# The first 256 rows of a row-mean kernel: one load with two rows a partition instead of two loads with one, and means interleaved on chip

## The chip, the cores and the metric

One core of one Trainium2 chip. The metric is the device time of one execution in microseconds. A "run" below is one execution; a median is over the runs named.

## The reference

```python
def setup_inputs():
    batch, seq, dim = 32, 512, 1024
    return {"x": np.random.randn(batch, seq, dim).astype(np.float32)}

def reference(x):
    return np.mean(np.maximum(x, 0), axis=-1).astype(np.float32)
```

So 16,384 rows of 4 KB (67.11 MB) are read, and one number per row is written.

## The kernel before

Each row's ReLU and sum is one instruction, on ScalarE for even rows and on VectorE for odd ones, so the loads hold whole rows (only the last row of each partition comes in column pieces). The 256 first rows are treated apart, as two loads of 128 rows. Of the others each partition owns 126 consecutive ones, which come in seven loads of 16 rows a partition (8 MB each, in three buffers), then in shrinking pieces.

```python
    xfirst, xmain = xf[:2 * P, :].rearrange("(c p) d -> p c d", c=2), xf[2 * P:, :]
    ...
    for t in range(full):                       # full = 7, issued from SyncE
        buf_free(t)                             # waits for load t-3 to be consumed
        if t in (0, 2):
            c = t // 2
            load(c - 2, row0[:, c, :], xfirst[:, c, :])                 # 512 KB, 4 KB packets
        load(t, bufs[t % BUFS][:, :, :], xr[:, t * NB:(t + 1) * NB, :]) # 8 MB, 64 KB packets
        if t == BUFS + 2:
            nc.sync.wait_ge(first, 2)
            for c in range(2):                  # two stores of four 128-byte runs
                nc.sync.dma_start(
                    out=outfirst[c * P:(c + 1) * P].rearrange("(q i) -> q i", i=32), in_=turned0[c:P:32, :],
                ).then_inc(stored, 16)
    ...
    for t in range(full):                       # ScalarE and VectorE
        if t in (0, 2):
            c = t // 2
            nc.scalar.wait_ge(loaded[c - 2], 16)
            done = nc.scalar.activation(out=row0[:, c, :], in_=row0[:, c, :], func=ACT.Relu, scale=inv,
                                        accum_out=mean0[:, c:c + 1])
            if c == 1:
                done.then_inc(first, 1)
                nc.vector.wait_ge(first, 1)
                nc.vector.transpose(turned0[:, :], mean0[:, :]).then_inc(first, 1)
        rows(t, bufs[t % BUFS], 0, NB, t * NB)
    ...
    issue_ahead_of_entry_barrier(nc, 2)         # the first two loads are issued before the entry barrier
```

The entry barrier is the point at the program's start at which the engines wait for one another; the helper in the last line moves the first loads in front of it.

## Time and profile before

| | before |
|---|---|
| time, median of the first 3 runs | 161.39 us (161.09 to 161.4) |
| span in the profile | 159.8 us |
| VectorE, ScalarE busy | 46%, 44% |
| mean rate out of HBM over the span | 420 GB/s |

The lines on which the bound is read stand in the prediction. This is the timeline of SyncE's queue in the kernel before (start us, us, what is issued; merged lines):

```profile
0.00 0.39 SPq L109 DMA_DIRECT2D row<-in_x_dram  x1
0.43 1.82 SPq L109 DMA_DIRECT2D rows<-in_x_dram  x2
2.30 0.43 SPq L109 DMA_DIRECT2D row<-in_x_dram  x1
...
72.53 1.20 SPq L127 DMA_DIRECT2D out_dram<-turned  x2
```

The first 512 KB are issued at once and load 0 at 0.43 us. The second 512 KB follow at 2.30, between loads 1 and 2. And this is the DMA view:

```profile
GB/s 394 525 263 525 476 312 525 410 377 525 394 525 263 525 476 312 525 427 361 525 377 410 525 312 476 525 263 525 525 263 525 525 263 525 361 394 427 416 407 112
DMA packets 2608, 67.18 MB, mean 420 GB/s; under 512 B 560, under 2 KB 816, under 8 KB 1328
```

### The profile page before, as it was taken

Reading aid. Unit: us, or ns where it says so; the run is one execution under the profiler, and the core shown is the slowest. Engines: PE = TensorE matmul, PEld = TensorE weight load, DVE = VectorE, ACT = ScalarE, POOL = GpSimd, SP = SyncE. Lnnn points to the kernel's source line nnn. Section 1 sums busy time; section 2 is a strip of 40 time slices with the busy share of each in tenths; the row PEclk is TensorE's granted clock in tenths of the full one; section 3 lists DMA queues with packets and bytes.
Section 4 is the critical chain, followed back from the end, with each engine's and each line's share of the span. In section 5 each row is a group of like instructions: output and inputs, shape, how many; then the busy total and the mean of one; then the engine's idle time right before and its main releaser. Section 6 shows DMA issues by size and latency. Waiting matters only on the chain. (4 is left out here: it accounts for less than half of the span.)

```text
span 159.8 us, 350 instructions
## 1 busy us (share of the span) xinstructions
DVE 73.1 (46%) x131; ACT 70.3 (44%) x133; POOL 1.3 (1%) x9
## 2 busy tenths in 40 slices
DVE  0000029900499002990049800597007950089995
ACT  1400029800499002980049600595007930089974
POOL 1000000000000000000000000000000000000001
DMA  9969979989996997998989979969969969899993
GB/s 394 525 263 525 476 312 525 410 377 525 394 525 263 525 476 312 525 427 361 525 377 410 525 312 476 525 263 525 525 263 525 525 263 525 361 394 427 416 407 112
DMA packets 2608, 67.18 MB, mean 420 GB/s; under 512 B 560, under 2 KB 816, under 8 KB 1328
## 3 DMA queue, kind: packets, MB, share of 16 engines
q1 hardware_dynamic: 2608, 67.18, 98.0%
HBM read 67.11 MB, written 0.07 MB: 420 GB/s over the span
## 5 line engine op out<-in xcount | busy, mean ns | idle before, releaser
L20 DVE TENSOR_SCALAR_CACHE_REDUCE rows<-rows 128x1024 f32<-128x1024 f32 (+1 forms) x63 | 71.9, 1208 | 84.5 <-DMA rows<-in_x_dram 84.5
L15 ACT ACTIVATE rows<-rows 128x1024 f32<-128x1024 f32 (+1 forms) x63 | 65.2, 1034 | 83.9 <-DMA rows<-in_x_dram 83.8
L15 ACT ACTIVATION_READ_ACCUMULATOR rows<-rows 128x1 f32 x63 | 11.7, 186 | 0.0
L20 DVE DVE_READ_ACCUMULATOR rows<-rows 128x1 f32 x63 | 5.2, 83 | 0.0
L169 ACT ACT_TABLE_LOAD x1 | 1.3, 1283 | 3.4 <-DMA row<-in_x_dram 3.4
L169 ACT ACTIVATE row<-row 128x1024 f32<-128x1024 f32 x2 | 2.1, 1048 | 0.0
L159 POOL TENSOR_SCALAR res<-sums 128x112 f32<-128x112 f32 (+1 forms) x2 | 0.5, 244 | 153.9 <-DVE rows L20 153.9
L15 ACT ACTIVATE last<-last 128x512 f32<-128x512 f32 x1 | 0.6, 629 | 0.0
L20 DVE TENSOR_SCALAR_CACHE_REDUCE last<-last 128x256 f32<-128x256 f32 x1 | 0.4, 420 | 0.3 <-DMA last<-in_x_dram 0.3
L203 DVE SCALAR_TENSOR_TENSOR last<-last,scale 128x258 f32<-128x258 f32 x1 | 0.4, 428 | 0.1
L169 ACT ACTIVATION_READ_ACCUMULATOR row<-row 128x1 f32 x2 | 0.4, 186 | 0.0
L175 DVE STREAM_TRANSPOSE turned<-mean 128x32 f32<-128x32 f32 x1 | 0.2, 214 | 0.3 <-ACT row L169 0.3
L144 POOL MEMSET scale<- 128x258 f32 x1 | 0.3, 313 | 0.0
L193 POOL TENSOR_SCALAR res<-part 128x1 f32<-128x1 f32 x1 | 0.3, 265 | 0.5 <-DVE rows L20 0.5
L15 ACT ACTIVATION_READ_ACCUMULATOR last<-last 128x1 f32 x1 | 0.2, 186 | 0.0
L143 POOL MEMSET mean<- 128x32 f32 x1 | 0.1, 125 | 1.5 <-POOLq L55 1.5
L241 POOL MEMSET const-bfloat16-1.0<- 128x1 bf16 x1 | 0.1, 101 | 0.0
L241 POOL MEMSET const-uint8-127<- 128x1 uint8 x1 | 0.1, 101 | 0.0
L241 POOL MEMSET const-float32-0.0<- 128x1 f32 x1 | 0.1, 98 | 0.2 <-issue 0.2
L241 POOL MEMSET const-float32-1.0<- 128x1 f32 x1 | 0.1, 98 | 0.0
L20 DVE DVE_READ_ACCUMULATOR last<-last 128x1 f32 x1 | 0.1, 83 | 0.0
L203 DVE DVE_READ_ACCUMULATOR last<-last,scale 128x1 f32 x1 | 0.1, 82 | 0.0
## 6 DMA issues: line engine op xcount, KB each, us to landing
rows<-in_x_dram SPq DMA_DIRECT2D x1, 3072.0 KB, 36.7
rows<-in_x_dram SPq DMA_DIRECT2D x1, 2048.0 KB, 41.2
row<-in_x_dram SPq DMA_DIRECT2D x2, 512.0 KB, 22.3
rows<-in_x_dram SPq DMA_DIRECT2D x1, 1024.0 KB, 43.2
rows<-in_x_dram SPq DMA_DIRECT2D x1, 512.0 KB, 44.0
last<-in_x_dram SPq DMA_DIRECT2D x1, 256.0 KB, 44.3
last<-in_x_dram SPq DMA_DIRECT2D x2, 128.0 KB, 44.0
rows<-in_x_dram SPq DMA_DIRECT2D x7, 48.7
```

Of the source, the lines that this page charges most:

```text
L15: return nc.scalar.activation(out=src, in_=src, func=ACT.Relu, accum_out=acc)
L20: return nc.vector.tensor_scalar(out=src, in0=src, scalar1=0.0, scalar2=init, op0=ALU.max, op1=ALU.add, accum_out=acc,)
L143: nc.gpsimd.memset(mean0[:, :], 0.0)
L144: nc.gpsimd.memset(scale[:, :], inv).then_inc(pool, 1)
L159: nc.gpsimd.tensor_scalar(out=res[:, lo:hi], in0=sums[:, lo:hi], scalar1=inv, scalar2=0.0, op0=ALU.mult, op1=ALU.add,).then_inc(pool, 1)
L169: done = nc.scalar.activation(out=row0[:, c, :], in_=row0[:, c, :], func=ACT.Relu, scale=inv, accum_out=mean0[:, c:c + 1],)
L175: nc.vector.transpose(turned0[:, :], mean0[:, :]).then_inc(first, 1)
L193: nc.gpsimd.tensor_scalar(out=res[:, J - 2:J - 1], in0=part[:, 0:1], scalar1=part[:, 1:2], scalar2=inv, op0=ALU.add, op1=ALU.mult,).then_i ...
L203: nc.vector.scalar_tensor_tensor(out=last[:, 768:], in0=last[:, 768:], scalar=0.0, in1=scale[:, :], op0=ALU.max, op1=ALU.mult, accum_out=r ...
L241: nc = _bacc.Bacc("TRN2", target_bir_lowering=False, num_devices=1)
```

## The change

The intent: fewer and larger transfers. Partition p takes rows 2p and 2p+1, so both lie together in memory, and one load of 1 MB in packets of 8 KB replaces two of 512 KB in packets of 4 KB. The means then come in pairs, so after VectorE's transpose GpSimd interleaves them, and one store of four 256-byte runs replaces two stores of four 128-byte runs.

```diff
-    xfirst, xmain = xf[:2 * P, :].rearrange("(c p) d -> p c d", c=2), xf[2 * P:, :]
+    xfirst, xmain = xf[:2 * P, :].rearrange("(p c) d -> p c d", c=2), xf[2 * P:, :]
...
-        if t in (0, 2):
-            c = t // 2
-            load(c - 2, row0[:, c, :], xfirst[:, c, :])
+        if t == 0:
+            load(-1, row0[:, :, :], xfirst)
         load(t, bufs[t % BUFS][:, :, :], xr[:, t * NB:(t + 1) * NB, :])
-        if t == BUFS + 2:
-            nc.sync.wait_ge(first, 2)
-            for c in range(2):
-                nc.sync.dma_start(
-                    out=outfirst[c * P:(c + 1) * P].rearrange("(q i) -> q i", i=32), in_=turned0[c:P:32, :],
-                ).then_inc(stored, 16)
+        if t == BUFS:
+            nc.sync.wait_ge(first, 3)
+            nc.sync.dma_start(
+                out=outfirst.rearrange("(q i) -> q i", i=64), in_=runs0[0:P:32, :, :],
+            ).then_inc(stored, 16)
...
+    nc.scalar.wait_ge(loaded[-1], 16)
+    for c in range(2):
+        done = nc.scalar.activation(
+            out=row0[:, c, :], in_=row0[:, c, :], func=ACT.Relu, scale=inv, accum_out=mean0[:, c, 0:1],
+        )
+    done.then_inc(first, 1)
+    nc.vector.wait_ge(first, 1)
+    nc.vector.transpose(turned0[:, :, :], mean0[:, :, :]).then_inc(first, 1)
+    nc.gpsimd.wait_ge(first, 2)
+    nc.gpsimd.tensor_copy(out=runs0[:, :, :].rearrange("p i c -> p c i"), in_=turned0[:, :, :]).then_inc(first, 1)
     for t in range(full):
-        (the same for t in (0, 2), one row each)
         rows(t, bufs[t % BUFS], 0, NB, t * NB)
```

Cut: the larger tiles, one load semaphore fewer, and the final wait for three stores in place of four.

More of the change, by code (lines that the diff above doesn't have):

```diff
@@ L88 @@
     scale = sbuf("scale", P, D // 4 + 2)
-    row0, mean0, turned0 = sbuf("row0", P, 2, D), sbuf("mean0", P, 32), sbuf("turned0", P, 32)
-    loaded = [nc.alloc_semaphore(f"loaded{i}") for i in range(full + len(row_pieces) + len(col_pieces) + 2)]
+    row0, mean0 = sbuf("row0", P, 2, D), sbuf("mean0", P, 2, 32)
+    turned0, runs0 = sbuf("turned0", P, 2, 32), sbuf("runs0", P, 32, 2)
+    loaded = [nc.alloc_semaphore(f"loaded{i}") for i in range(full + len(row_pieces) + len(col_pieces) + 1)]
     act, dve, pool = (nc.alloc_semaphore(n) for n in ("act", "dve", "pool"))
@@ L140 @@
         c, i = c + w, i + 1
-    nc.gpsimd.memset(mean0[:, :], 0.0)
+    nc.gpsimd.memset(mean0[:, :, :], 0.0)
     nc.gpsimd.memset(scale[:, :], inv).then_inc(pool, 1)
@@ L164 @@
     nc.vector.wait_ge(pool, 1)
-    for t in range(full):
-        if t in (0, 2):
-            c = t // 2
-            nc.scalar.wait_ge(loaded[c - 2], 16)
-            done = nc.scalar.activation(
-                out=row0[:, c, :], in_=row0[:, c, :], func=ACT.Relu, scale=inv, accum_out=mean0[:, c:c + 1],
-            )
-            if c == 1:
-                done.then_inc(first, 1)
-                nc.vector.wait_ge(first, 1)
-                nc.vector.transpose(turned0[:, :], mean0[:, :]).then_inc(first, 1)
+    nc.scalar.wait_ge(loaded[-1], 16)
[8 more added lines that the diff above has]
+    nc.gpsimd.tensor_copy(out=runs0[:, :, :].rearrange("p i c -> p c i"), in_=turned0[:, :, :]).then_inc(first, 1)
+    for t in range(full):
         rows(t, bufs[t % BUFS], 0, NB, t * NB)
@@ L223 @@
     nc.switch_bb("rows_end")
-    nc.sync.wait_ge(stored, 64).then_inc(stored, -64)
+    nc.sync.wait_ge(stored, 48).then_inc(stored, -48)
     issue_ahead_of_entry_barrier(nc, 2)
```

## The prediction

> **What bounds the kernel now.** I started with the head of the page and the busy slices, to see which engine could be the bound.
>
> ```profile
> span 159.8 us, 350 instructions
> DVE 73.1 (46%) x131; ACT 70.3 (44%) x133; POOL 1.3 (1%) x9
> ...
> DMA  9969979989996997998989979969969969899993
> ...
> HBM read 67.11 MB, written 0.07 MB: 420 GB/s over the span
> ```
>
> No engine is half busy, while the DMA row reads 9 or nearly so from the first slice to the last but one. The dips to 6 are long packets counted in one slice. The kernel is a stream of 67.11 MB out of HBM, and the two arithmetic engines wait for it. The view of waits says the same:
>
> ```profile
> DVE rows L20 <- DMA rows<-in_x_dram: 84.5, 7, 23.0
> ACT rows L15 <- DMA rows<-in_x_dram: 83.8, 9, 17.0
> ```
>
> Columns: total us, times, longest. VectorE waits 84.5 us in seven waits, one for each 8 MB load. The chain that ended last is of no use here: it stops after half a microsecond, at the last VectorE instruction. So I read the landings of the loads from the timeline, where the first instruction after an idle stretch starts when its load has landed:
>
> ```profile
> 3.44 1.28 ACT L169 ACT_TABLE_LOAD   x1 [3.44 <-DMA row<-in_x_dram]
> ...
> 23.00 1.22 DVE L20 TENSOR_SCALAR_CACHE_REDUCE rows<-rows 128x1024 f32<-128x1024 f32 x1 [23.00 <-DMA rows<-in_x_dram]
> 42.24 1.22 DVE L20 TENSOR_SCALAR_CACHE_REDUCE rows<-rows 128x1024 f32<-128x1024 f32 x1 [10.04 <-DMA rows<-in_x_dram]
> 62.86 1.22 DVE L20 TENSOR_SCALAR_CACHE_REDUCE rows<-rows 128x1024 f32<-128x1024 f32 x1 [10.91 <-DMA rows<-in_x_dram]
> 82.21 1.22 DVE L20 TENSOR_SCALAR_CACHE_REDUCE rows<-rows 128x1024 f32<-128x1024 f32 x1 [10.14 <-DMA rows<-in_x_dram]
> ```
>
> The later ones start at 101.57, 120.92 and 140.25 in the same view. Where nothing but an 8 MB load lies between two landings the step is 19.35 us, and 8.389 MB / 19.35 us = 433.5 GB/s. Between 42.24 and 62.86 lies also the second small load of 512 KB (0.524 MB): the step is 20.62 us, 1.27 more. At 433.5 GB/s its bytes alone are 1.21 us, so its being a transfer of its own, in 4 KB packets, costs about **0.06 us**. The span is a head (about 1 us to the first packet), some 156 us of stream, and a tail of 2 to 3 us (last reduction, last store).
>
> **What the Trainium skill says.**
> 1. "DMA: Bandwidth & Descriptors", section "Where 436 GB/s comes from": the fabric into SBUF tops out at 435.2 GB/s, and HBM gives one core about 358. The trace agrees with the first: 433.5. It does not show the second as a limit for this one core.
> 2. Same page, "Why small descriptors are slow (HBM only)": each packet carries a fixed overhead. The records of single packets in the trace agree and give its size: a 4 KB packet takes 159 ns, 8 KB 309, 16 KB 612, 64 KB 2418. From 8 KB to 64 KB that is 0.0368 ns a byte, so about 8 ns of each packet are fixed.
> 3. Same page, "Rules for kernel authors": at least 1 MiB per DMA for bandwidth. That rule would favour the change (512 KB becomes 1 MB), but in this trace the 512 KB load lost only 0.06 us, because other loads stand in the queue on both sides of it.
> 4. "VectorE: DVE Perf Modes", "The three transpose paths": VectorE turns 32x32 blocks independently. The trace has the one used, 128x32 in 214 ns; the changed one has two such columns of blocks.
>
> **The change, part by part.**
>
> *Loads.* Two loads of 512 KB, 128 packets of 4 KB each, become one of 1 MB with 128 packets of 8 KB. The bytes are the same. Each of 16 engines moves 8 packets of 309 ns instead of 16 of 159: 2472 against 2544 ns, **0.07 us less** on the stream, which sets the end. One load fewer also saves one completion write of 9 ns per engine, 0.01 us. The issue of the second load (0.43 us of SyncE at 2.30) is off the path, since the queue holds an 8 MB load by then.
>
> *Order.* All 1 MB now lies ahead of load 0, so loads 0 and 1 land about 1.20 us later (24.1 and 43.4), and from load 2 on everything lands about 0.08 us earlier (62.78, 82.13, ...). Their buffers come free 1.2 us later: the issue of load 3, at 32.30 now, moves to about 33.5. Load 3's turn on the DMA engines comes at 62.8, so 29 us of slack remain.
>
> *Arithmetic on the first rows.* Two ScalarE activations (1.05 us + 0.19 each) stay. They move together, after a landing at about 4.6 and the table load of 1.28, so they end near 8.4 us. Then VectorE's transpose (one more column of blocks than 214 ns: I take 0.25), then a new GpSimd copy of 128x64. GpSimd's 128x112 instruction takes 286 ns and its 128x12 one 201, so 0.85 ns a column and 0.25 us for 64. The larger memset takes perhaps 0.03 us more. All is done by about 9.2 us, with VectorE and ScalarE idle until load 0 lands at 24.1. Before, the second activation and the transpose sat at 50.6 to 52.0, also in idle time. On the path: **0**.
>
> *Stores.* Two stores of four 128-byte runs become one of four 256-byte runs, issued after load 3 (near 33.8) instead of after load 5 (72.5). In the packet records the old ones ran at 120.05 to 120.2, behind load 5, at 13 ns a packet. The step from 120.92 to 140.25 that contains them is 19.33, no longer than others. Saving at most 0.02 us, if those engines are the slow ones. SyncE is spared one issue of about 0.6 us, off the path. The wait for the means (three signals) is met 24 us before SyncE comes to it.
>
> *Tail.* Load 6 and the pieces behind it shift by the same 0.08 us. VectorE works without a break from load 6's landing to 157.0 and then waits 0.3 us for the last column pieces. Both sides of that near-tie move together, so the shift passes through to the end.
>
> Sum: 0.07 + 0.01 + up to 0.02, about **0.1 us less**: 161.39 becomes **161.3 us**. That is 0.06%, below the spread of the three runs before (161.09 to 161.4).
>
> **Rivals.**
> - *The first load delays everything.* If load 0's landing 1.2 us later were not given back at load 2, the time would be 162.6. Against it: total bytes are unchanged and the queue never empties (steps of 19.35 throughout). For it only that load 0's landing does move.
> - *The new chain ScalarE, VectorE, GpSimd, SyncE becomes a wait that blocks the queue.* SyncE issues load 4 behind that store. Against: done near 9 us, needed at 33.8; even then load 4 has until 82. Cost 0. To cost anything it would have to take over 70 us.
> - *A full fixed cost per transfer is saved.* Were some 2 us of set-up and receipt exposed for each load, the gain would be 1 to 2 us, about 160.0. Against: the measured 0.06 us above.
> - *The ramp at the start.* The first packets of 4 KB take 355 to 638 ns instead of 159, while the rate builds up. If with 8 KB packets the ramp is better or worse used, I would put it at 0.1 to 0.2 us either way, 161.1 to 161.5. This is the largest real doubt, and it is as large as the effect.
>
> **Range and chances.** The mechanism gives 161.3; the ramp and the run-to-run spread of 0.3 us are larger than the gain. The range that should hold it 8 times in 10 is 160.9 to 161.7. A change of 2% is 3.2 us: nothing in the rivals reaches it. Faster 0.01, within 2% 0.98, slower 0.01.
>
> **What would show it.** Right: 2456 packets instead of 2608 (128 of data, 4 of stores and 20 completion writes fewer) and under 8 KB 1048 instead of 1328; loads 0 and 1 landing at about 24.1 and 43.4, loads 2 to 6 about 0.08 us earlier than before; steps between landings still 19.35; the copy on GpSimd over by 10 us; load 3 issued near 33.5 without the queue running dry; the waits of VectorE for loads still near 84 us. Wrong: load 2 landing later than 62.9, a step other than 19.35 where the store now runs (load 3 to load 4), or SyncE held at its wait for the means. A span that differs by over 0.4 us would mean that the head or the tail does something that I have not seen.

## The result, and the profile after

After: **161.25 us**, median of 6 runs (161.15 to 161.34). Before, in the runs beside it: 161.16 us, median of 6 (160.98 to 161.4). Ratio 1.0003, 95% interval 0.999 to 1.0016: the same. A ratio here is the mean time of one kernel's runs over that of the other's of the same rounds, so it is not quite the ratio of the medians quoted.

The page and the DMA view of the kernel after:

```profile
span 159.9 us, 349 instructions
DVE 73.1 (46%) x131; ACT 70.3 (44%) x133; POOL 1.6 (1%) x10
GB/s 248 539 525 262 525 525 262 525 525 262 525 508 279 525 459 328 525 361 426 525 263 525 525 262 525 525 262 525 525 262 525 525 262 525 361 394 426 414 407 114
DMA packets 2456, 67.18 MB, mean 420 GB/s; under 512 B 536, under 2 KB 792, under 8 KB 1048
```

The packet counts are the predicted ones (2456 and 1048). The first GB/s slice falls from 394 to 248, which looks like a much slower start and is not one. The single-packet records show that the first 16 packets of 64 KB start from 2.5 us on before and from 4.2 on after; in a slice of 4.0 us 16 such packets are 262 GB/s. The row of slices is too coarse here for packets of 2.4 us; the landings tell more. The timeline of the kernel after, first its beginning, then the instructions that start as loads land:

```profile
8.51 0.24 DVE L171 STREAM_TRANSPOSE turned<-mean 128x64 f32<-128x64 f32 x1 [8.51 <-ACT row L166]
8.82 0.24 POOL L173 COPY runs<-turned 128x64 f32<-128x64 f32 x1 [6.49 <-DVE turned L171]
...
24.22 1.22 DVE L20 TENSOR_SCALAR_CACHE_REDUCE rows<-rows 128x1024 f32<-128x1024 f32 x1 [15.47 <-DMA rows<-in_x_dram]
43.56 1.22 DVE L20 TENSOR_SCALAR_CACHE_REDUCE rows<-rows 128x1024 f32<-128x1024 f32 x1 [10.13 <-DMA rows<-in_x_dram]
62.92 1.22 DVE L20 TENSOR_SCALAR_CACHE_REDUCE rows<-rows 128x1024 f32<-128x1024 f32 x1 [10.16 <-DMA rows<-in_x_dram]
82.27 1.22 DVE L20 TENSOR_SCALAR_CACHE_REDUCE rows<-rows 128x1024 f32<-128x1024 f32 x1 [10.14 <-DMA rows<-in_x_dram]
```

The means are ready at 9.06 us. The steps between landings are 19.34 to 19.36 us. Load 0's first instruction starts at 24.22 and not at 24.1, and load 2's at 62.92, which is 0.06 us later than before and not 0.08 earlier. SyncE's queue shows no hold-up: load 3's issue ends at 0.44 + 33.40 = 33.84, and the store follows at once.

```profile
0.44 33.40 SPq L110 DMA_DIRECT2D rows<-in_x_dram  x4
33.90 0.64 SPq L126 DMA_DIRECT2D out_dram<-runs  x1
```

**How the start is measured below.** A load lands when the last of the 16 DMA engines has written its share. The trace records each engine's landing, so each load has a mean over the engines and a last one. The mean shows how much stream time was lost; the last decides when the arithmetic may start, and it decides the end: an engine that is behind hardly catches up (in the table the distance from mean to last at load 0 is still there at load 6, within 0.05 us in all profiles but head_2k, where 1.5 us become 1.3). The table has all runs (us from the start of the span; ratio to the kernel before in the same rounds).

| run | median | ratio (95%) | load 0 mean / last | load 2 mean / last | load 6 mean / last |
|---|---|---|---|---|---|
| before | 161.16 | | 22.59 / 22.86 | 62.58 / 62.84 | 139.99 / 140.23 |
| before_again | 161.30 | 1.0001 (0.9988 to 1.0015) | 22.60 / 22.81 | 62.59 / 62.79 | 140.23 / 140.44 |
| after | 161.25 | 1.0003 (0.999 to 1.0016) | 24.00 / 24.20 | 62.70 / 62.90 | 140.11 / 140.31 |
| after_again | 161.17 | 0.9994 (0.9981 to 1.0007) | 23.98 / 24.20 | 62.70 / 62.92 | 140.10 / 140.32 |
| store_early | 161.28 | 0.9999 (0.9986 to 1.0013) | 24.03 / 24.31 | 62.75 / 63.00 | 140.16 / 140.42 |
| head_16k | 161.21 | 0.9999 (0.9984 to 1.0015) | 23.93 / 24.16 | 62.63 / 62.87 | 140.04 / 140.30 |
| one_load_mid | 161.65 | 1.0022 (1.0008 to 1.0035) | 21.67 / 22.29 | 62.84 / 63.44 | 140.26 / 140.84 |
| one_load_mid_n1 | 161.62 | 1.0035 (1.0021 to 1.0048) | 21.65 / 22.49 | 62.83 / 63.65 | 140.24 / 141.04 |
| one_load_4k | 161.67 | 1.0025 (1.0012 to 1.0038) | 24.47 / 24.63 | 63.18 / 63.34 | 140.60 / 140.75 |
| two_loads_head | 162.08 | 1.0054 (1.004 to 1.0068) | 24.49 / 25.10 | 63.22 / 63.90 | 140.62 / 141.27 |
| two_loads_head_n2 | 162.02 | 1.0065 (1.0052 to 1.0079) | 24.62 / 25.01 | 63.32 / 63.71 | 140.73 / 141.13 |
| before_n1 | 162.44 | 1.0078 (1.0064 to 1.0092) | 23.75 / 24.43 | 63.73 / 64.41 | 141.18 / 141.85 |
| after_n1 | 162.62 | 1.0089 (1.0074 to 1.0104) | 24.97 / 25.84 | 63.67 / 64.54 | 141.08 / 141.95 |
| head_2k | 163.54 | 1.0149 (1.0133 to 1.0164) | 23.29 / 24.82 | 63.30 / 64.80 | 141.00 / 142.30 |

### The profile page after: what moved, and what is told of

Same layout as the page of the kernel before. It is cut to its first block, busy times and chain, and to the rows that moved or that the text cites. A ratio compares the mean times of both kernels' runs of the same rounds, so it can differ in the third digit from the quotient of the medians.

```text
span 159.9 us, 349 instructions
## 1 busy us (share of the span) xinstructions
DVE 73.1 (46%) x131; ACT 70.3 (44%) x133; POOL 1.6 (1%) x10
## 2 busy tenths in 40 slices
DMA packets 2456, 67.18 MB, mean 420 GB/s; under 512 B 536, under 2 KB 792, under 8 KB 1048
## 3 DMA queue, kind: packets, MB, share of 16 engines
q1 hardware_dynamic: 2456, 67.18, 97.8%
## 5 line engine op out<-in xcount | busy, mean ns | idle before, releaser
L20 DVE TENSOR_SCALAR_CACHE_REDUCE rows<-rows 128x1024 f32<-128x1024 f32 (+1 forms) x63 | 71.9, 1208 | 76.3 <-DMA rows<-in_x_dram 76.3
L166 ACT ACTIVATE row<-row 128x1024 f32<-128x1024 f32 x2 | 2.1, 1048 | 0.0
```

Of the source, the lines that this page charges most:

```text
L20: return nc.vector.tensor_scalar(out=src, in0=src, scalar1=0.0, scalar2=init, op0=ALU.max, op1=ALU.add, accum_out=acc,)
```

## The experiments

The predicted saving of 0.08 us has to be somewhere between load 0's landing and load 2's. From before to after the mean landing of load 0 moves by 24.00 - 22.59 = 1.41 us, where the packets account for 8 x (309 - 159) ns = 1.20. So about 0.2 us are lost at the start, on top of the packets. The first theory was that this is systematic and belongs to the 8 KB packets; its rival, that it is the chance of one run. All kernels gave correct results.

### The repeats: after_again and before_again

Both are the unchanged kernels, run again.

> The changed kernel once more, for the spread of its ramp and a tighter ratio. Theory S (the start eats the gain): in the profile of after, half of the engines' first 8 KB packets start at 1.7 us instead of 1.0 and the other half take 1.0 to 1.3 us, so load 0 lands 1.34 us later than before instead of the 1.20 predicted, and load 2 lands 0.06 us later (62.92). If S is systematic, load 0 lands at 24.2 again (within 0.05), load 2 at 62.9, and the ratio to before is 1.000 to 1.001. Rival N (chance of one run): load 0 lands at 24.1 or earlier, load 2 at 62.8 or earlier, ratio 0.999 to 1.000.

> The kernel before as a run of its own, for the repeat of its start. If the start belongs to the kernel (S, P): the first 4 KB packets take 0.35 to 0.64 us on most engines, the 16 engines have load 0 at 22.6 in the mean and 22.85 at the last (0.05 either way), and load 6 at 139.99 and 140.23. If starts differ from run to run (N), the means differ by 0.1 us or more, as much as between before and after. Ratio 1.000 within 0.1%: the size of the noise.

The start repeats: load 0's mean is 24.00 and 23.98 after, 22.59 and 22.60 before, so the loss at the start (0.21 and 0.18 us against the 1.20) belongs to the kernel and not to chance. These two repeats ran on different chips; store_early and before_again, on one chip, differ by 24.03 - 22.60 = 1.43, so the chip isn't the reason either. The ratio of after_again lies below 1, outside what that theory expected, and inside the noise.

The end does not repeat. In before_again load 6's mean is 140.23 and not 139.99. The mean landings of that run step by 19.46 and 19.45 us into loads 4 and 5, the others by 19.35. A run can lose 0.2 us in mid-stream, which is more than all that the change does.

### The saving by itself: one_load_mid

```diff
-        if t == 0:
+        if t == 2:
             load(-1, row0[:, :, :], xfirst)
...
-        if t == BUFS:
+        if t == BUFS + 2:
```

ScalarE's two rows, the transpose and the copy move ahead of `rows(2, ...)` too.

> The single 1 MB load in 8 KB packets, moved to just ahead of load 2, where the queue is full; its chain and its store in the places they had before. It measures the predicted saving without the start: the step from load 1 to load 2 should be 19.35 + 2.42 + at most 0.06 = 21.77 to 21.83 us if 8 KB packets cost in the stream what single packets of that size take (309 ns times 8 = 2.47). The program now starts with 64 KB packets. S1: the ramp is worse or no better than with 8 KB, load 0 lands at 21.6 or later (22.88 less the 1.27 of a 512 KB load would be 21.61). If large packets don't hurt the start: 21.5 or earlier, and the time is 0.1 us below before.

The stretches from landing to landing, of one_load_mid (columns: stretch, length, busy VectorE, ScalarE and GpSimd with counts, clock, DMA share, GB/s; a packet is counted whole where it starts, which is how a share can exceed 1):

```profile
22.43:41.63 19.20, 9.21 (x16) 9.64 (x17) 0.00 (x0) 1.00 0.94 407
41.63:63.47 21.84, 9.46 (x18) 10.51 (x21) 0.24 (x1) 1.00 1.06 458
63.47:82.81 19.34, 9.20 (x16) 8.42 (x16) 0.00 (x0) 1.00 1.00 434
```

The step with the 1 MB load is 21.84 us, also in the means (41.00 to 62.84), so the load costs 21.84 - 19.35 = 2.49 us in the stream. One 512 KB load costs 20.626 - 19.352 = 1.274 there (before's means), two 2.55. **The saving exists: 0.06 us**, 0.08 predicted. It repeats: the step is 21.84 again in one_load_mid_n1 below, and 20.63 in before_again. The start is the other half of the result. With 64 KB packets at the very beginning load 0 lands at 21.67 in the mean and 22.29 at the last engine, 0.62 behind the mean where the two main kernels have 0.20 to 0.27. Load 0 did not come by 21.5, and the kernel is 0.2% slower than before.

### Is it the size of the packets or of the load: one_load_4k and two_loads_head

Theory S1 says that 8 KB packets make the start slow, S2 that a single load of 1 MB does, whatever its packets. one_load_4k keeps one load, but leaves 8 unused elements between the two rows of a partition, so that it goes in 4 KB packets:

```diff
-    row0, mean0 = sbuf("row0", P, 2, D), sbuf("mean0", P, 2, 32)
+    row0, mean0 = sbuf("row0", P, 2, D + 8), sbuf("mean0", P, 2, 32)
...
-            load(-1, row0[:, :, :], xfirst)
+            load(-1, row0[:, :, :D], xfirst)
```

> The same single load of 1 MB at the start, but its destination rows are 8 elements apart from each other, so it goes in 256 packets of 4 KB. Theory S1 (8 KB packets make the ramp slow): all 16 engines start within 0.4 us of each other as before, their first packets take 355 to 640 ns, load 0 lands at 24.10 to 24.15, and load 2 near 62.85, although the packets cost 0.07 us more in all. Theory S2 (one load of 1 MB ramps slowly, whatever its packets): half of the engines start 0.6 us late, load 0 lands at 24.3. Rival N: 24.17 and 62.86, from packet cost alone. Time within 0.1% of before in each.

two_loads_head keeps two loads of 4 KB packets, both at the start:

```diff
-            load(-1, row0[:, :, :], xfirst)
+            for c in range(2):
+                load(c - 2, row0[:, c, :], xfirst[:, c, :])
...
-    issue_ahead_of_entry_barrier(nc, 2)
+    issue_ahead_of_entry_barrier(nc, 3)
```

> The first rows still come interleaved and all at the start, but as two loads of 512 KB in 4 KB packets (all three first loads issued ahead of the entry barrier). S1 and S2 both expect the start of before: 16 engines within 0.4 us, load 0 at 24.10 to 24.15, load 2 near 62.85. If a 1 MB head costs something else than its packets (a slower second transfer, a start-up time during which everything is slow), load 0 lands at 24.2 or later here too. Against one_load_4k it tells S1 from S2. Time within 0.1% of before.

Load 0 lands at 24.63 and 25.10 at the last engine, and the kernels are 0.25% and 0.54% slower than before. The landings of one_load_4k fit no expectation; those of two_loads_head meet only the third (24.2 or later, "something else"), and neither time is within the 0.1%. For one_load_4k the queue's timeline names a confounder:

```profile
0.00 0.69 SPq L110 DMA_DIRECT2D row<-in_x_dram  x1
0.74 33.55 SPq L110 DMA_DIRECT2D rows<-in_x_dram  x4
```

Issuing the load with gaps takes 0.69 us instead of 0.39, and its first packet starts at 1.47 instead of 1.03. So the run cannot cleanly separate packet size from a late start. It gives a hint: no packet starts between 1.65 and 2.13 us, so six or seven of the 16 engines begin about 0.65 us after the others, as eight do in the run "after" (1.02 to 1.10, then 1.68 to 1.83), and as S2 expected. Less the 0.44 us, load 0's mean would be 24.03 (an estimate, if a late start shifts everything alike), close to the 24.00 with 8 KB packets. That points away from the packet size, but does not show it.

In two_loads_head the first packets go well (222 ns in the mean over the first 16 records, 436 before). Then from 2.25 to 2.75 us the 16 engines together move some 160 GB/s instead of 434, while packets of 4 KB take up to 681 ns. By then some 270 to 350 KB are through, so the dip lies inside the first load and not at the hand-over to the second. The first load itself is late: it lands at 3.67 in the mean and 3.94 at the last engine, against 3.10 and 3.37 before, though it has the same size and packets. ScalarE's first wait, in the kernel before and in two_loads_head, shows it:

```profile
3.44 1.28 ACT L169 ACT_TABLE_LOAD   x1 [3.44 <-DMA row<-in_x_dram]
4.01 1.28 ACT L167 ACT_TABLE_LOAD   x1 [4.01 <-DMA row<-in_x_dram]
```

Afterwards the engines are spread: the last is 0.61 us behind the mean, and still 0.65 behind at load 6. The expected clean test of S1 against S2 failed; what it showed is that a first load of 512 KB in 4 KB packets can go well or badly, depending on something besides its own size. Two things differ from before: the rows (every second one, where before they lie together) and the load behind it (another 512 KB, where before it is 8 MB). No run separates these two. A third difference, a third load issued ahead of the barrier, is taken away in the next section.

### Does the issue of the next load disturb the first: after_n1, before_n1, one_load_mid_n1, two_loads_head_n2

The next theory, C, was that the next load's issue, at 0.4 to 0.9 us, slows the first packets. In these four only one load (two in the last) is issued ahead of the entry barrier:

```diff
-    issue_ahead_of_entry_barrier(nc, 2)
+    issue_ahead_of_entry_barrier(nc, 1)
```

(3 becomes 2 in two_loads_head_n2.)

> The changed kernel with only its first load issued ahead of the entry barrier; load 0 is issued after it, near 1.9 us instead of 0.44. Theory C (contention at the start: the issue of the next load, with the descriptors it makes, slows the first packets of the load that is under way): the first 8 KB packets take about 0.5 us instead of 0.85 to 1.3, the mean landing of load 0 over the 16 engines moves from 24.0 to 23.7 to 23.8, and the time falls by 0.2 to 0.3 us, ratio to before about 0.998. Rival P (the slow start belongs to packets of 8 KB): the first packets as before, load 0 at 24.0 in the mean, time unchanged. If load 0's descriptors come too late (first packets of load 0 after 4.3 us), the time rises.

> The same step in the kernel before: load 0 is issued near 1.9 us, when the first 512 KB are over at 2.75. C: the 4 KB packets between 1.9 and 2.3 us (up to 347 ns now) fall to 159, but load 0's first packets may start late, near 3.0, a gap of 0.2 to 0.3 us that gives it all back: time 0 to 0.3 us longer than before. P: packets unchanged, the same gap. The run shows whether a 512 KB head is long enough to hide the later issue, which the 1 MB head should be.

> The kernel with the 1 MB load ahead of load 2, with only load 0 ahead of the barrier and load 1 after it. C: the first 64 KB packets fall from 3.18 us in the mean to about 2.8 or less, load 0's mean landing from 21.67 to 21.3 or earlier and the time falls by 0.3 us or more. P: first packets as before, time unchanged (161.65).

> The kernel with two 512 KB loads at the head, both ahead of the barrier, and load 0 after it (1.9 us instead of 0.90). C: the dip of the rate from 2.0 to 3.0 us (159 GB/s at its lowest) goes or moves later and gets smaller, the spread of the engines at load 0 (0.61 us from mean to last) falls under 0.4, and the time falls by 0.4 us or more from 162.08. P or another cause: dip and spread stay, time within 0.15 us of 162.08.

C as the cause of the slow start is refuted. In one_load_mid_n1 load 0's mean is 21.65 against 21.67 and the time 161.62; in two_loads_head_n2 the time is 162.02 and the first load still lands at 3.61 in the mean; the dip gets smaller (205 GB/s at its lowest) and the spread falls to 0.39, as C expected, but the time doesn't. In after_n1 the 1 MB load lands at 4.60 in the mean, against 4.64 to 4.69 in the three profiles with two loads ahead: less than 0.1 us of the loss goes with the next issue. Beyond that, the two main kernels lose 1.3 us and more. The timeline of after_n1, queue and landing:

```profile
1.45 34.04 SPq L110 DMA_DIRECT2D rows<-in_x_dram  x4
...
25.86 1.22 DVE L20 TENSOR_SCALAR_CACHE_REDUCE rows<-rows 128x1024 f32<-128x1024 f32 x1 [17.11 <-DMA rows<-in_x_dram]
```

Load 0 is issued at 1.45 us and its first packets start between 3.86 and 5.55, with only 12 of 16 engines at work at 4.5 us. Those packets take 3.1 us in the mean instead of 2.42. In before_n1 they start between 2.85 and 4.03. So the issue of load 0 one microsecond later costs more than one, in both kernels: its packets start unevenly and are slow. Why they start so late after the issue, no run shows. My expectation that 1 MB at the head would hide the later issue was wrong.

### The chain in front of the queue: store_early

```diff
+        if t == 1:
+            nc.sync.wait_ge(first, 3)
+            nc.sync.dma_start(out=outfirst..., in_=runs0[0:P:32, :, :]).then_inc(stored, 16)
         load(t, bufs[t % BUFS][:, :, :], xr[:, t * NB:(t + 1) * NB, :])
-        if t == BUFS:
-            (the same)
```

> The changed kernel with the store of the first means moved from behind load 3 to ahead of load 1: SyncE stands at its wait until the GpSimd copy is over near 9.1 us and issues load 1 only then. The rival of the chain that blocks the queue, made as hard as it can be. I expect it to cost nothing, since load 0 keeps the DMA engines busy until 24: load 1 issued near 9.9 us, landing at 43.5, step from load 0 19.35, time within 0.1% of the changed kernel (161.2). If load 1 needed more than 14 us of lead, the step would be longer than 19.4.

Waits of SyncE's queue in store_early, then its timeline:

```profile
SPq L125 <- POOL runs L173: 7.3, 1, 7.3
```

```profile
9.20 0.64 SPq L125 DMA_DIRECT2D out_dram<-runs  x1
9.89 102.96 SPq L110 DMA_DIRECT2D rows<-in_x_dram  x10
```

SyncE now really stands 7.3 us at that wait, and load 1 is issued at 9.89. The step from load 0 to load 1 is still 19.36 in the mean (24.03 to 43.39), and the time is unchanged. So the rival "the new chain blocks the queue" is refuted with a harder case than the change: this wait, over 14 us before load 0 lands, costs nothing.

### Does the start get worse with larger packets: head_16k and head_2k

Theory P: a cold first packet costs more the larger it is. head_16k puts four rows of load 0 in front, in 16 KB packets; head_2k cuts the first 512 KB of the kernel before into two column halves of 2 KB packets.

```diff
(head_16k, from after)
+            lo = 4
+            load(-2, bufs[0][:, :lo, :], xr[:, :lo, :])
             load(-1, row0[:, :, :], xfirst)
+        load(t, bufs[t % BUFS][:, lo:, :], xr[:, t * NB + lo:(t + 1) * NB, :])
(head_2k, from before)
-            load(c - 2, row0[:, c, :], xfirst[:, c, :])
+                load(-3, row0[:, c, :D // 2], xfirst[:, c, :D // 2])
+                load(-2, row0[:, c, D // 2:], xfirst[:, c, D // 2:])
```

In both, three loads are issued ahead of the barrier.

> The changed kernel with the first four rows of load 0 ahead of everything, as a load of 2 MB in 16 KB packets; the 1 MB load and the rest of load 0 follow, all three ahead of the barrier. P (a cold first packet costs more the larger it is): the first packets of the 16 engines end 1.25 us or later after their start (612 ns warm), an excess between the 0.76 us of 64 KB and the 0.6 to 0.85 of 8 KB; the stream's deficit at 5 us is 1.9 to 2.0 us (before 1.64, after 1.88), time 0.1 to 0.3 us above the changed kernel. If only 8 KB packets or only the shape of the first load are to blame: deficit 1.6 to 1.7, time at or below before.

> The kernel before with its first 512 KB cut into two loads of 256 KB in 2 KB packets, both and load 0 ahead of the barrier. P: the cold first packets end 0.35 us or less after their start in the mean (before 0.44, with 4 KB), so the rate rises earlier. The time should not gain: the second load's first packets are due at about 1.9 us, and in the runs with two 512 KB loads at the head the second one was not ready before 2.1 to 2.9, so I expect a dip of the rate near 2 us as there, and a time 0.3 us or more above before.

From the single-packet records: the mean time at which the 16 engines end their first packet, less what such a packet takes in the running stream, is the moment at which a warm engine would have started it. ("Cold" and "warm" are names for the slow first packets and the later ones. The records name no engine; which packet is an engine's first is worked out from starts and ends, good to some 0.03 us.)

| first packets | profiles | warm start equivalent, us |
|---|---|---|
| 2 KB | head_2k | 1.22 |
| 4 KB | before, before_again | 1.43, 1.29 |
| 8 KB | after, after_again, store_early | 1.84, 1.82, 1.84 |
| 16 KB | head_16k | 1.64 |
| 64 KB | one_load_mid, one_load_mid_n1 | 1.98, 1.97 |

The 8 KB start is 0.4 to 0.55 us later than the 4 KB one in all three profiles. (The n1 runs, with a later second issue, are not in the table; worked out alike they have some 1.40 with 4 KB and 1.7 with 8 KB.) (The kernels before lose part of that again up to 7 us, in their first 64 KB packets, which take 2528 ns in the first round against 2419 after; the balance at load 0 is the 0.2 us.) But 16 KB start earlier than 8 KB, so **P is not a law of the packet's size**: head_16k was expected under P to lose 0.1 to 0.3 us against the changed kernel and lost none. What is special about the 8 KB load stays open. It differs from the 16 KB one also in its addresses (one contiguous megabyte against pieces 126 rows apart), and no run separates the two. head_2k did start earliest, as expected. The hand-over from its first to its second small load shows no gap (320 to 365 GB/s from 1.75 to 2.5 us). Then the rate dipped, to 235 GB/s near 3 us, when some 520 KB were through: the second small load ends unevenly (2.73 to 3.91), load 0's first packets start between 2.42 and 3.86 and take 3.07 us in the mean instead of 2.42. The last engine fell 1.5 us behind the mean, and the time rose by 1.5%. Load 0 is issued at 0.91 us here instead of 0.43, and packets and loads are smaller; no run separates these.

## Why the prediction was right

161.25 lies 0.05 us from the forecast of 161.3, and "within 2%" had the chance of 0.98. That the number is so close is partly luck. The forecast took off 0.1 us from 161.39, the median of three runs; the same kernel had 161.16 in the six runs beside the result. So the gain of 0.1 us was not seen; that the change is far too small to matter was right, and for the reasons given, but for one term. Point by point:

- **The bound** was right. The steps between landings are 19.35 us in both kernels, and wherever the start or the stream loses time, the end loses about as much.
- **The packet term** (0.07 us, and 0.01 for one load fewer) was nearly right: 0.06 together in one_load_mid.
- **Load 0's and load 1's 1.20 us** were too little: 1.41 in the mean, 1.38 in the repeat. The ramp, which I had set at nothing in the sum and at 0.1 to 0.2 us either way among the rivals, costs about 0.2 us. That is the mis-sized term, and it is larger than the gain. Two slips stand in the prediction's text. The first 4 KB packets take 218 to 638 ns, not 355 to 638. And 23.00 + 1.20 is 24.2 and not 24.1: the 24.1 fits the landing, 22.86, which the first VectorE instruction follows 0.14 us later there (ScalarE's starts at 22.88). From instruction to instruction load 0 seems to move by the forecast 1.22; the last engine's landing moves by 1.34.
- So **"from load 2 on everything lands about 0.08 us earlier" was wrong**. By the test that I had set (later than 62.9 is wrong) load 2's 62.92 fails it narrowly. In the mean over the engines it is 0.12 us later (62.70 against 62.58), in the repeats 0.11. The engines' spread decides how much of it the last one shows: 0.06 us between the first two profiles, 0.13 between the repeats.
- **The arithmetic** was right: transpose 0.245 us (0.25 estimated), copy 0.240 (0.25), all over at 9.06 (9.2), nothing on the path. VectorE's waits changed in the view only because the transpose now splits the first one (76.3 + 8.5 us).
- **Stores and queue** were right: four packets at 18 ns, no step longer for them, load 3 issued near 33.5, and store_early makes the wait harmless even before load 1.
- **The tail** passed the shift through, as said: from load 6's last landing to the end of the span it is 19.55 us before and 19.57 after.

The expected gain of 0.1 us was therefore not simply hidden. It was made in mid-stream, where the second small load is gone, and given back at the start (by 8 us, when the first 64 KB packets are over). Whether the whole is then 0.06% faster or slower cannot be told: the two ratios are 1.0003 and 0.9994, the intervals are 0.0026 wide, and the kernel before against itself gave 1.0001.

## What to carry to other kernels

In a kernel that is one unbroken stream of loads, count what a transfer costs between two landings before merging transfers: here a 512 KB load in a full queue cost 0.06 us more than its bytes, so merging two could not matter. The first microseconds are another matter. In the two main kernels load 0 issued one microsecond later cost 0.8 and 0.9%, and splitting the first 512 KB in two (with smaller packets, and load 0 issued 0.5 us later) cost 1.5%, so try the order and the sizes of the first loads by measurement; why one start is slower than another stays open here. Look at the last of the DMA engines and not only at the mean, since an engine that started behind stayed behind to load 6 in every profile.

## What the Trainium skill lacked or had wrong

- "DMA: Bandwidth & Descriptors", section "Rules for kernel authors", asks for at least 1 MiB a DMA. It does not say what a smaller one loses between other loads in a full queue: here a 512 KB load lost 0.06 us (1.27 us for 0.524 MB against 1.21 at 433.5 GB/s).
- Same page, section "Latency and other measured facts", gives about 600 ns to the first byte for the hardware queues. The first packet here started at 1.03 us, 0.64 us after the end of the 0.39 us issue, which agrees if it is counted from there. It lacks what follows: the 16 engines' first packets start 0.3 to 1.4 us apart (1.03 to 1.37 before, 1.03 to 2.44 in one_load_mid_n1), take longer than later ones (8 KB 0.5 to 1.0 us in the mean over three profiles, against 309 ns), and in after_n1 a load issued at 1.45 us found its last engine only at 5.55, where the load ahead of it had landed by 4.85.
- No page that I read says how the issue time of a load from SyncE grows: 0.69 us with gaps in the destination (256 packets) against 0.39 without (128 packets) for the same 1 MB. Whether the gaps or the number of packets matter, no run separates.
